# Two key tiles moved behind the first block substitution, one gate tile behind the second, and a later step for the first head's blocks

## The chip, the cores and the metric

The kernel runs on one core of one Trainium2 chip. The metric is the device time of one execution in microseconds (us). TensorE is called PE here, VectorE DVE, ScalarE ACT, GpSimd POOL and SyncE SP, as in the profile.

## The reference, cut to what matters

One decoder layer on 512 tokens of width 2048, all in float32:

```python
u    = rms_norm(x)
proj = u @ w_in                        # 2048 -> 6160 columns
conv = 8 groups of 128 channels: GLU, causal depthwise conv (31 taps), LayerNorm, swish
dn   = 8 heads of 128: short conv (4 taps) + SiLU on q, k, v; gated delta rule in chunks of 64;
       RMSNorm, times silu(z)
h1   = x  + concat(conv, dn) @ w_out
y    = rms_norm(h1 + relu(rms_norm(h1) @ w_up)^2 @ w_down)
```

For each head and chunk the delta rule needs the inverse of a unit lower triangular matrix made of the keys: `t_mat = (I + strict_lower(beta * k k^T * decay))^-1`. With it come `u = t_mat (beta v)` and `w = t_mat (beta k exp(g))`, and then a short recurrence over the chunks. The kernel takes chunks of 128 instead of 64.

## The kernel before, in words

Tokens lie in 4 tiles of 128. Every weight is split into a high and a low part (`whi` by ACT, `wlo` by DVE, lines 157 and 158), and each product is three matmuls (lines 163 to 165). A column tile of the input projection (`in_tile`, 128 columns by 512 tokens) is 48 matmuls of 512 columns. In the trace it is called `pin_` and a letter: a and g for a conv group, q, v, z, k for a head.

The input projection is a list of steps, `ORDER` (line 28). `K3` is head 3's key tile and starts `head_keys(3)`; `I0` inverts the blocks of heads 0 to 3 (`invert_blocks`); `C0` is conv group 0 (tiles a0 and g0); `H0` is delta head 0 (tiles q0 and v0, then z0 for the gate). What follows a tile runs as a generator beside the later tiles. Each `yield n` means: go on after n advances, and `in_tile` makes one advance after every 6 matmuls, 8 to a tile. Starting a second generator of the same kind finishes the one before it (`drain`).

`head_keys` (lines 442 to 481) puts on POOL one product `ug` (line 448, the other half is DVE's), the mask of `dec` (line 459) and a power, `kn` (line 480). The two `ug` of a head feed two matmuls into `pd`; `ug` has a single buffer, so that each next one waits for the matmul of the one before.

`invert_blocks` (lines 483 to 508) writes the four heads' key matrices `na` to DRAM and reads them back as 64 blocks of 32 by 32 (`inv_a`, four DMAs). It runs 31 steps of forward substitution on POOL, two instructions each (lines 503 and 505, 62 in all, on w(j+1) elements with w from 31 to 1), and writes the result to DRAM (`blk_out`). All its DMAs stand in POOL's queue.

`delta_head` (lines 510 to 653) first fetches its four diagonal blocks: a DMA `yc` on POOL, a masked copy `y` on POOL, and four 32-row transposes into `xx` on DVE (line 527). Then follow the short convs of q and v (lines 424 to 435, on ACT and DVE), after `Y_PTQ` = 10 advances the transposes `ptq`, `ptv`, `ptk` on PE, after 13 more (`Y_PX`, first head of a batch) or 1 more (`Y_PX2`, the others) the products `pp`, `pz`, `pp`, `pz` that put the 32-blocks together, then `pw`, `pqk` and the chain over the four chunks.

`conv_group` (lines 379 to 422) is 30 multiply-adds `cacc` on DVE, each of which needs the one before (line 390). They begin when both tiles are there (`chh`), and the PE transposes `cpt` follow them.

Each engine takes its instructions in the order in which they stand in its queue. A scheduler puts them there by program order and `high_priority` offsets and by its own estimate of when each is ready; `pin` keeps the small PE instructions among themselves in program order. A waiting instruction holds up all that stand behind it on its engine.

Of the kernel before, what the change touches and what calls it, by code (L numbers as in the profile page):

```python
# [24 lines left out]
FB = 512  # L25
NROWS = 21
HB = 4
ORDER = "A0 K0 K1 K2 K3 I0 C0 H0 C1 H1 C2 K4 H2 K5 C3 H3 K6 K7 I1 C4 H4 C5 H5 C6 H6 C7 H7"
EPS = 1e-6
DRAW = 5  # L30

# [1 line left out]

NPK, TAPS, Y_PTK, Y_PX2 = 2, 3, 6, 1
S1, S2, S3 = 1, 1, 1
Y_CPT, Y_CPB, Y_PX, Y_POT, Y_PTQ = 14, 8, 13, 4, 10
C_CONF = 0
C_GATE = 1024
C_Q = 2048
# [7 lines left out]
def tile_hybrid_block(ctx: ExitStack, tc: tile.TileContext, x, norm1_w, w_in, b_glu, dw_w, dw_b,  # L47
# [27 lines left out]
    def tt(tag, name, shape=(P, NT, P), dtype=F32, bufs=1):  # L75
        return tmp.tile(list(shape), dtype, tag=tag, name=name, bufs=bufs)
# [4 lines left out]
    def bc(ap):  # L81
        return ap.unsqueeze(2).to_broadcast([P, NT, P])
# [296 lines left out]
    def conv_group(g, pa, pgt):  # L379
        th = tt("c0", f"cth{g}")  # L380
        nc.scalar.activation(fl(th), pgt, AF.Tanh, bias=hgate_c[:, g:g + 1], scale=0.5)
        av = tt("c1", f"cav{g}")
        nc.scalar.activation(fl(av), pa, AF.Identity, bias=bglu_c[:, g:g + 1])
        hh = tt("c2", f"chh{g}", (P, SEQ))
        nc.vector.scalar_tensor_tensor(hh, fl(th), 1.0, fl(av), ALU.add, ALU.mult)
        acc = tt("c3", f"cacc{g}", (P, SEQ))
        nc.scalar.activation(acc, hh, AF.Identity, scale=dw_cols[:, WCONV - 1, g:g + 1],  # L387
                             bias=dwb_c[:, g:g + 1])
        for j in range(1, WCONV):
            nc.vector.scalar_tensor_tensor(acc[:, j:], hh[:, :SEQ - j],  # L390
                                           dw_cols[:, WCONV - 1 - j, g:g + 1], acc[:, j:],
                                           ALU.mult, ALU.add)
# [12 lines left out]
        nc.vector.tensor_scalar(vs, mv[:, :, 1], EPS, None, ALU.add)
        rs = small.tile([P, NT], F32, tag="crs", bufs=2, name=f"crs{g}")
        nc.gpsimd.tensor_tensor(rs, vs, neg_half[:, 0:NT], ALU.pow)
        hn = tt("c4", f"chn{g}")
        for t in range(NT):
            nc.vector.tensor_scalar(hn[:, t], pt[:, t], mv[:, t, 0:1], rs[:, t:t + 1],  # L410
                                    ALU.subtract, ALU.mult)
        yield Y_CPB
        pb = bank(f"cpb{g}")
        for t in range(NT):
            pin(nc.tensor.transpose(pb[:, t], hn[:, t], ident))
        xh = tt("c1", f"cxh{g}")
        nc.scalar.activation(xh, pb, AF.Identity, scale=hlng_c[:, g:g + 1],
                             bias=hlnb_c[:, g:g + 1])
        th2 = tt("c0", f"cth2{g}")
        nc.scalar.activation(th2, xh, AF.Tanh)  # L420
        mixes[g] = row(f"mix{g}")
        nc.vector.scalar_tensor_tensor(mixes[g], fl(th2), 1.0, fl(xh), ALU.add, ALU.mult)

    def short_conv(ps, which, h, tag, acc):
# [9 lines left out]
        nc.vector.scalar_tensor_tensor(acc, th, 1.0, acc, ALU.add, ALU.mult)  # L434
        return acc

    def square_sums(ps, ss, h, name):
        for t in range(NT):
            junk = tt("sj", f"{name}j{h}{t}", (P, P))
            nc.scalar.activation(junk, ps[:, t], AF.Square, accum_out=ss[:, t:t + 1])  # L440

    def head_keys(h, pk):

        pd = bank(f"pd{h}")

        def decay_sums(i):
            ug = tt("ug", f"ug{h}{i}", dtype=F32R)
            (nc.gpsimd, nc.vector)[i].tensor_mul(ug, upper.unsqueeze(1).to_broadcast([P, NT, P]),
                                 bc(glog_split[:, i, :, h]))
            pin(nc.tensor.matmul(fl(pd), lhsT=strict_r, rhs=fl(ug), start=(i == 0), stop=(i == 1)))  # L450

        decay_sums(0)
        k = row(f"k{h}", (P, NT, P))
        short_conv(pk, 1, h, "k", k)
        yield 2
        decay_sums(1)
        dec = row(f"dec{h}", (P, NT, P))
        nc.scalar.activation(dec, pd, AF.Exp)
        nc.gpsimd.tensor_mul(dec, dec, upper.unsqueeze(1).to_broadcast([P, NT, P]))
        yield Y_PTK  # L460
        ptk = bank(f"ptk{h}")
        for t in range(NT):
            pin(nc.tensor.transpose(ptk[:, t], k[:, t], ident))
        kss = small.tile([P, NT], F32, tag="kss", bufs=HB + 1, name=f"kss{h}")
        square_sums(ptk, kss, h, "k")
        nc.vector.tensor_scalar(kss, kss, EPS, None, ALU.add)
        br = small.tile([P, 2, NT], F32, tag="br", bufs=HB + 1, name=f"br{h}")
        nc.vector.reciprocal(br[:, 0], kss)
        nc.vector.tensor_mul(br[:, 0], br[:, 0], beta[:, :, h])
# [12 lines left out]

    def invert_blocks(bt, keys):
# [182 lines left out]
    for op in ORDER.split():  # L666
        kind, r = op[0], int(op[1])
        if kind == "A":

            pabT = ps_mm.tile([P, SEQ], F32, tag="mm", name="pabT")  # L670
            pk = ps_mm.tile([P, SEQ], F32, tag="mm", name="pin_k0")
            ws = [in_weights(C_K, j, "k0", nc.gpsimd, True) for j in range(2)]
            for i in range(2):
                toks = slice(256 * i, 256 * i + 256)
                decay_products(pabT, toks)
                if i:
                    beta, glog_split, eg = decay_columns(pabT)
                for k in range(KT):
                    w = ws[k // 8]
                    mm3(pk[:, toks], (w[0][:, k % 8], w[1][:, k % 8]),  # L680
                        (uT[k][0][:, toks], uT[k][1][:, toks]), start=(k == 0), stop=(k == KT - 1))
        elif kind == "K":
            if r:
                pk = in_tile(C_K + r * P, f"k{r}", nc.gpsimd if r < NPK else nc.vector)
            start(f"key{r}", head_keys(r, pk))
        elif kind == "I":
            drain("key")
            blocks[r] = invert_blocks(r, keys[r * HB:(r + 1) * HB])
        elif kind == "C":
# [318 lines left out]
```

## Time and profile before

| | us |
|---|---|
| median of 3 runs (2214.61 to 2217.39) | 2215.02 |
| the profiled execution | 2217.25 |
| its span | 2215.2 |
| PE busy | 2162.8 |
| DVE busy | 1537.8 |
| ACT busy | 816.0 |
| POOL busy | 226.2 |

The first 40 us load and normalize x. The mixers (ORDER's steps) take until about 720 us, the output projection until about 920 us, the MLP the rest. A change of ORDER touches the stretch from 90 to 720 us alone. PE is the engine to follow: where it has work, the time goes on at its pace, and what another engine costs is seen as PE idle time or as PE at the lower of its two clocks.

### The profile page before, as it was taken

Reading aid. Unit: us, or ns where it says so; the run is one execution under the profiler, and the core shown is the slowest. Engines: PE = TensorE matmul, PEld = TensorE weight load, DVE = VectorE, ACT = ScalarE, POOL = GpSimd, SP = SyncE. Lnnn points to the kernel's source line nnn. Section 1 sums busy time; section 2 is a strip of 40 time slices with the busy share of each in tenths; the row PEclk is TensorE's granted clock in tenths of the full one; section 3 lists DMA queues with packets and bytes.
Section 4 is the critical chain, followed back from the end, with each engine's and each line's share of the span. In section 5 each row is a group of like instructions: output and inputs, shape, how many; then the busy total and the mean of one; then the engine's idle time right before and its main releaser. Section 6 shows DMA issues by size and latency. Waiting matters only on the chain.

```text
span 2215.2 us, 25987 instructions
## 1 busy us (share of the span) xinstructions
PE 2162.8 (98%) x10073; PEld 1791.7 (81%) x10073; DVE 1537.8 (69%) x1956; ACT 816.0 (37%) x1349; POOL 226.2 (10%) x265
## 2 busy tenths in 40 slices
PE   6998999998999999999999999999999999999998
PEld 5877888877888788888888888888888888888886
DVE  6586687586679323477777767767768767768775
ACT  5333433432435323333423424324323423333343
POOL 3382111282100000000000000000000000000000
PEclk9999999999999999999999999999999999999999
DMA  6323233232233633233333233333343333332332
GB/s 164 105 77 75 78 87 90 80 83 73 77 81 86 190 97 94 76 96 117 92 105 114 86 116 103 88 122 95 95 119 95 100 115 95 106 111 89 115 117 84
DMA packets 189768, 220.66 MB, mean 100 GB/s; under 512 B 9901, under 2 KB 108622, under 8 KB 189646
## 3 DMA queue, kind: packets, MB, share of 16 engines
q1 hardware_dynamic: 188238, 215.34, 33.4%
q0 software_dynamic: 1408, 3.67, 0.6%
q8 instruction: 79, 1.29, 0.2%
q14 instruction: 43, 0.35, 0.1%
HBM read 212.17 MB, written 6.82 MB: 99 GB/s over the span
## 4 chain that ended last, share of the span: by engine, by line
PE 88%; POOL 6%; DVE 2%; DMA 2%; issue 1%; ACT 0%; SPq 0%; POOLq 0%; DVEq 0%; ACTq 0%
PE pu L165 10%; PE pu L164 10%; PE pu L163 10%; PE px L164 5%; PE px L165 5%; PE px L163 5%; PE py L164 4%; PE py L163 4%; PE py L165 4%; PE po L163 3%; PE po L165 3%; PE po L164 3%; POOL inv_g L505 2%; POOL inv_t L503 2%; PE pin_k L163 1%
## 5 line engine op out<-in xcount | busy, mean ns | idle before, releaser
L165 PE MATMUL pu<-v_h,wlo_u 128*128 128x512 f32 x1024 | 398.8, 389 | 0.0
L163 PE MATMUL pu<-v_h,whi_u 128*128 128x512 f32 x1024 | 398.4, 389 | 0.0
L164 PE MATMUL pu<-v_l,whi_u 128*128 128x512 f32 x1024 | 398.4, 389 | 0.0
L840 DVE TENSOR_TENSOR wlo_d<-wd,whi_d 128x1024 fp32r<-128x1024 f32 x180 | 218.3, 1219 | 249.8 <-ACT whi_d L839 249.8
L839 ACT CAST whi_d<-wd 128x1024 fp32r<-128x1024 f32 x180 | 189.6, 1054 | 454.7 <-PE pu L164 289.4
L165 PEld LDWEIGHTS pu<-v_h,wlo_u 128*128 128x128 f32 x1024 | 192.2, 188 | 40.1 <-issue 0.2
L163 PEld LDWEIGHTS pu<-v_h,whi_u 128*128 128x128 f32 x1024 | 192.3, 188 | 40.0 <-issue 0.2
L164 PEld LDWEIGHTS pu<-v_l,whi_u 128*128 128x128 f32 x1024 | 192.3, 188 | 39.8
L157 ACT CAST whi_u<-wraw_u 128x1024 fp32r<-128x1024 f32 x128 | 134.8, 1053 | 198.5 <-PE py L165 75.1
L390 DVE SCALAR_TENSOR_TENSOR cacc<-chh,dw_cols,cacc 128x511 f32<-128x511 f32 (+14 forms) x240 | 196.1, 817 | 8.4 <-ACT cacc L387 5.1
L163 PE MATMUL px<-whi_d,sh 128*128 128x512 f32 x480 | 186.7, 389 | 0.0
L164 PE MATMUL px<-wlo_d,sh 128*128 128x512 f32 x480 | 186.7, 389 | 0.0
L165 PE MATMUL px<-whi_d,sl 128*128 128x512 f32 x480 | 186.7, 389 | 0.0
L158 DVE TENSOR_TENSOR wlo_u<-wraw_u,whi_u 128x1024 fp32r<-128x1024 f32 x128 | 155.8, 1217 | 41.2 <-ACT whi_u L157 41.2
L857 DVE TENSOR_TENSOR h<-px,h 128x1024 f32<-128x1024 f32 x120 | 146.5, 1221 | 28.7 <-PE px L165 28.7
L163 PE MATMUL py<-whi_d,sh 128*128 128x512 f32 x360 | 140.0, 389 | 0.0
L164 PE MATMUL py<-wlo_d,sh 128*128 128x512 f32 x360 | 140.0, 389 | 0.0
L165 PE MATMUL py<-whi_d,sl 128*128 128x512 f32 x360 | 140.0, 389 | 0.0
L176 POOL TENSOR_TENSOR rs_rf<-rs_sf,neg_half 128x1 f32<-128x1 f32 x4 | 2.2, 543 | 1309.1 <-DVE rs_sf L174 1309.1
L857 DVE TENSOR_TENSOR h<-py,h 128x1024 f32<-128x1024 f32 x90 | 109.8, 1220 | 22.6 <-PE py L165 22.6
L163 PEld LDWEIGHTS px<-whi_d,sh 128*128 128x128 f32 x480 | 90.1, 188 | 18.7
L165 PEld LDWEIGHTS px<-whi_d,sl 128*128 128x128 f32 x480 | 90.1, 188 | 18.7
(304 smaller groups left out, 4125.5 us busy)
## 6 DMA issues: line engine op xcount, KB each, us to landing
wraw_u<-in_w_mlp_up SPq DMA_DIRECT2D x128, 512.0 KB, 3.7
wd<-in_w_mlp_down SPq DMA_DIRECT2D x120, 512.0 KB, 3.7
wraw_o<-in_w_out SPq DMA_DIRECT2D x32, 512.0 KB, 4.2
wraw_k<-in_w_in SPq DMA_DIRECT2D x16, 512.0 KB, 4.4
wraw_a<-in_w_in SPq DMA_DIRECT2D x16, 512.0 KB, 3.9
wraw_g<-in_w_in SPq DMA_DIRECT2D x16, 512.0 KB, 3.9
wraw_q<-in_w_in SPq DMA_DIRECT2D x16, 512.0 KB, 3.9
wraw_v<-in_w_in SPq DMA_DIRECT2D x16, 512.0 KB, 4.0
```

The source lines that it names most:

```text
L157: nc.scalar.copy(hi, raw)
L158: sub.tensor_sub(lo, raw, hi.bitcast(F32))
L163: nc.tensor.matmul(ps, lhsT=sta[0], rhs=mov[0], start=start, stop=False, skip_group_check=more)
L164: nc.tensor.matmul(ps, lhsT=sta[0], rhs=mov[1], start=False, stop=False, skip_group_check=more)
L165: nc.tensor.matmul(ps, lhsT=sta[1], rhs=mov[0], start=False, stop=stop, skip_group_check=more)
L176: nc.gpsimd.tensor_tensor(rr, s, neg_half[:, 0:1], ALU.pow)
L390: nc.vector.scalar_tensor_tensor(acc[:, j:], hh[:, :SEQ - j], dw_cols[:, WCONV - 1 - j, g:g + 1], acc[:, j:], ALU.mult, ALU.add)
L503: nc.gpsimd.tensor_mul(tv, a[:, j:j + 1, j + 1:].to_broadcast([n, j + 1, w]), g[:, :j + 1, j:j + 1].to_broadcast([n, j + 1, w]))
L505: nc.gpsimd.tensor_add(g[:, :j + 1, j + 1:], g[:, :j + 1, j + 1:], tv)
L839: nc.scalar.copy(hi, src)
L840: nc.vector.tensor_sub(lo, src, hi.bitcast(F32))
L857: nc.vector.tensor_add(h, ps, h)
```

## The change

- In `ORDER`, K4 and K5 stand right behind I0 (before, they stood behind C2 and H2), so that their two tiles and their generators run beside the first substitution. A new step `Z4` (head 4's z tile) stands right behind I1; H4 then skips its own.
- The first head of a batch (heads 0 and 4, `late`) no longer fetches its blocks at its start. The fetch, now the function `block_inverse` with the same instructions, stands 6 advances (`Y_PX` = 6) behind `ptk`, and `pp` 4 advances (`Y_XX` = 4) behind that: 20 advances after the head's start where there were 23. The other heads are as before.
- `ahead()` raises the priority of some POOL instructions (`ug`, `dec`, `kn`, `rt`, `crs`; of `ug` DVE's half too) by 600. `kss`, `br` and `kn` have 6 buffers each instead of 5.

```diff
-ORDER = "A0 K0 K1 K2 K3 I0 C0 H0 C1 H1 C2 K4 H2 K5 C3 H3 K6 K7 I1 C4 H4 C5 H5 C6 H6 C7 H7"
+ORDER = "A0 K0 K1 K2 K3 I0 K4 K5 C0 H0 C1 H1 C2 H2 C3 H3 K6 K7 I1 Z4 C4 H4 C5 H5 C6 H6 C7 H7"
...
-Y_CPT, Y_CPB, Y_PX, Y_POT, Y_PTQ = 14, 8, 13, 4, 10
+Y_CPT, Y_CPB, Y_PX, Y_XX, Y_POT, Y_PTQ = 14, 8, 6, 4, 4, 10
...
+    def ahead():
+
+        return tc.high_priority(offset=600)
...
-        nc.gpsimd.tensor_mul(dec, dec, upper.unsqueeze(1).to_broadcast([P, NT, P]))
+        with ahead():
+            nc.gpsimd.tensor_mul(dec, dec, upper.unsqueeze(1).to_broadcast([P, NT, P]))
...
-    def delta_head(h, key, blocks, pq, pvv):
-        e_c, e_s, e_l = (eg[:, i, :, h] for i in range(3))
-        k, dec, na, kn, br = key
+    def block_inverse(h, blocks):
 
         y = tt("y", f"y{h}")
...
             nc.vector.transpose(xx[rows, :, col:col + 32], yc[rows])
-
+        return y, xx
+
+    def delta_head(h, key, blocks, pq, pvv):
+        e_c, e_s, e_l = (eg[:, i, :, h] for i in range(3))
+        k, dec, na, kn, br = key
+        late = h % HB == 0
+        if not late:
+            y, xx = block_inverse(h, blocks)
...
-        yield Y_PX if h % HB == 0 else Y_PX2
+        if late:
+            yield Y_PX
+            y, xx = block_inverse(h, blocks)
+            yield Y_XX
+        else:
+            yield Y_PX2
...
+        elif kind == "Z":
+            drain("head")
+            gates[r] = z_gate(in_tile(C_Z + r * P, f"z{r}"), r)
         else:
             pq = in_tile(C_Q + r * P, f"q{r}")
             pvv = in_tile(C_V + r * P, f"v{r}")
             start("head", delta_head(r, keys[r], blocks[r // HB], pq, pvv))
-            gates[r] = z_gate(in_tile(C_Z + r * P, f"z{r}"), r)
+            if gates[r] is None:
+                gates[r] = z_gate(in_tile(C_Z + r * P, f"z{r}"), r)
```

POOL's queue from the fetch of the first batch's blocks (`inv_a0`) on, before; the numbers in the names are head, batch and step:

```order
L495 DMA inv_a0_1043<-blk_in0_1041 16x32x32 x4
L503 TENSOR_TENSOR inv_t0_0_1055<-inv_a0_1043,inv_g0_1052 64x31
L505 TENSOR_TENSOR inv_g0_1052<-inv_g0_1052,inv_t0_0_1055 64x31
L503 TENSOR_TENSOR inv_t0_1_1058<-inv_a0_1043,inv_g0_1052 64x60
L505 TENSOR_TENSOR inv_g0_1052<-inv_g0_1052,inv_t0_1_1058 64x2x30
```

The same place now:

```order
L503 DMA inv_a0_1043<-blk_in0_1041 16x32x32
L454 TENSOR_TENSOR ug50_1324<-upper_128,gh_605 128x512
L503 DMA inv_a0_1043<-blk_in0_1041 16x32x32
L466 TENSOR_TENSOR dec4_1247<-dec4_1247,upper_128 128x512
L503 DMA inv_a0_1043<-blk_in0_1041 16x32x32 x2
L488 TENSOR_TENSOR kn4_1321<-kss4_1297,half_136 128x4
L511 TENSOR_TENSOR inv_t0_0_1055<-inv_a0_1043,inv_g0_1052 64x31
L513 TENSOR_TENSOR inv_g0_1052<-inv_g0_1052,inv_t0_0_1055 64x31
L511 TENSOR_TENSOR inv_t0_1_1058<-inv_a0_1043,inv_g0_1052 64x60
L454 TENSOR_TENSOR ug60_3582<-upper_128,gh_605 128x512
L513 TENSOR_TENSOR inv_g0_1052<-inv_g0_1052,inv_t0_1_1058 64x2x30
L511 TENSOR_TENSOR inv_t0_2_1061<-inv_a0_1043,inv_g0_1052 64x87
```

Instructions of heads 4 to 6 now stand among the fetch and the first steps; `dec5` follows the last row shown, and further back in the substitution stand `kn5` and the DMAs that write `na4` and `na5`.

DVE's queue about head 0's v (the last product, which writes the finished `v0`) and its block transposes (`xx0`), before:

```order
L434 SCALAR_TENSOR_TENSOR v0_1449<-vth0_1454,v0_1449 128x512
L390 SCALAR_TENSOR_TENSOR cacc0_1280<-chh0_1278,dw_cols_141,cacc0_1280 128x488
L390 SCALAR_TENSOR_TENSOR cacc0_1280<-chh0_1278,dw_cols_141,cacc0_1280 128x487
L390 SCALAR_TENSOR_TENSOR cacc0_1280<-chh0_1278,dw_cols_141,cacc0_1280 128x486
L390 SCALAR_TENSOR_TENSOR cacc0_1280<-chh0_1278,dw_cols_141,cacc0_1280 128x485
L158 TENSOR_TENSOR wlo_g11_1689<-wraw_g11_1686,whi_g11_1688 128x1024
L390 SCALAR_TENSOR_TENSOR cacc0_1280<-chh0_1278,dw_cols_141,cacc0_1280 128x484
L659 SCALAR_TENSOR_TENSOR z0_1523<-zth0_1521,pin_z0_1457 128x512
L390 SCALAR_TENSOR_TENSOR cacc0_1280<-chh0_1278,dw_cols_141,cacc0_1280 128x483
L527 STREAM_TRANSPOSE xx0_1435<-yc0_1432 32x4x32 x4
L390 SCALAR_TENSOR_TENSOR cacc0_1280<-chh0_1278,dw_cols_141,cacc0_1280 128x482
```

The same queue now, from the multiply-add on 497 columns on:

```order
L390 SCALAR_TENSOR_TENSOR cacc0_1500<-chh0_1498,dw_cols_141,cacc0_1500 128x497
L533 STREAM_TRANSPOSE xx0_1845<-yc0_1842 32x4x32
L390 SCALAR_TENSOR_TENSOR cacc0_1500<-chh0_1498,dw_cols_141,cacc0_1500 128x496
L533 STREAM_TRANSPOSE xx0_1845<-yc0_1842 32x4x32
L390 SCALAR_TENSOR_TENSOR cacc0_1500<-chh0_1498,dw_cols_141,cacc0_1500 128x495
L533 STREAM_TRANSPOSE xx0_1845<-yc0_1842 32x4x32
L390 SCALAR_TENSOR_TENSOR cacc0_1500<-chh0_1498,dw_cols_141,cacc0_1500 128x494
L158 TENSOR_TENSOR wlo_a11_1814<-wraw_a11_1811,whi_a11_1813 128x1024
L390 SCALAR_TENSOR_TENSOR cacc0_1500<-chh0_1498,dw_cols_141,cacc0_1500 128x493
L430 SCALAR_TENSOR_TENSOR v0_1659<-pin_v0_1578,sc_cols_140,v0_1659 128x511
```

Three of the four transposes of `xx0` now stand ahead of all of v0's instructions; the finished `v0` comes 8 rows after the last row shown.

DVE's queue at the same place of the second batch (head 4), now:

```order
L435 SCALAR_TENSOR_TENSOR v4_4291<-vth4_4296,v4_4291 128x512
L390 SCALAR_TENSOR_TENSOR cacc4_4132<-chh4_4130,dw_cols_141,cacc4_4132 128x488
L533 STREAM_TRANSPOSE xx4_4473<-yc4_4470 32x4x32
L390 SCALAR_TENSOR_TENSOR cacc4_4132<-chh4_4130,dw_cols_141,cacc4_4132 128x487
L533 STREAM_TRANSPOSE xx4_4473<-yc4_4470 32x4x32
L390 SCALAR_TENSOR_TENSOR cacc4_4132<-chh4_4130,dw_cols_141,cacc4_4132 128x486
```

Here the transposes still stand behind the finished `v4`; before, six multiply-adds, a weight part and z4 stood between them, as at head 0. On PE, `cpt4` now comes 36 matmuls after `ptk` of head 4 instead of 48 (36 of a5 and 12 of g5), and `cpb4`, the transposes of the normalized group, 16 matmuls after `cpt4` instead of 36.

## Rows read from the trace of the kernel before

**Rows 1.** PE's waits: what waited, for whom: us in total, times, longest.
```profile
PE cpt L398 <- DVE cacc L390: 11.1, 2, 5.7
PE ptv L548 <- DVE v L434: 10.4, 2, 5.3
```
**Rows 2.** PE's timeline, first batch: start us, us, what [idle before, releaser].
```profile
88.79 0.60 PE L463 MATMUL ptk<-ident,k 128*128 128x128 f32 x4
...
90.35 0.40 PE L163 MATMUL pin_a<-u_h,whi_a 128*128 128x512 f32 x1
...
103.22 0.39 PE L163 MATMUL pin_g<-u_h,whi_g 128*128 128x512 f32 x1
...
114.10 0.39 PE L163 MATMUL pin_q<-u_h,whi_q 128*128 128x512 f32 x1
...
149.47 0.60 PE L537 MATMUL ptq<-ident,q 128*128 128x128 f32 x4
155.15 1.12 PE L548 MATMUL ptv<-ident,v 128*128 128x128 f32 x4 [5.09 <-DVE v L434]
...
175.10 1.11 PE L398 MATMUL cpt<-ident,cacc 128*128 128x128 f32 x4 [5.37 <-DVE cacc L390]
...
185.28 1.00 PE L570 MATMUL pp<-xx,na 128*128 128x64 f32 x8
```
**Rows 3.** Five us after a wait: PE PEld DVE ACT POOL, PE clock, DMA share, GB/s.
```profile
155.00:160.00 5.00, 4.85 (x16) 4.18 (x17) 4.89 (x6) 4.36 (x19) 4.61 (x6) 0.50 0.31 92
```
**Rows 4.** PE's timeline, second batch.
```profile
490.06 1.12 PE L548 MATMUL ptv<-ident,v 128*128 128x128 f32 x4 [5.28 <-DVE v L434]
...
510.18 1.12 PE L398 MATMUL cpt<-ident,cacc 128*128 128x128 f32 x4 [5.72 <-DVE cacc L390]
...
520.07 1.00 PE L570 MATMUL pp<-xx,na 128*128 128x64 f32 x8
```
**Rows 5.** DVE's timeline, first batch.
```profile
116.44 0.94 DVE L385 SCALAR_TENSOR_TENSOR chh<-cth,cav 128x512 f32<-128x512 f32 x1
...
139.34 5.44 DVE L390 SCALAR_TENSOR_TENSOR cacc<-chh,dw_cols,cacc 128x497 f32<-128x497 f32 x5
...
154.02 1.08 DVE L434 SCALAR_TENSOR_TENSOR v<-vth,v 128x512 f32<-128x512 f32 x1
...
173.05 1.24 DVE L527 STREAM_TRANSPOSE xx<-yc 32x128 f32<-32x128 f32 x4 [10.55 <-DMA yc<-blk_out]
```
**Rows 6.** POOL's timeline: head 2's key instructions, then the first batch's substitution.
```profile
92.01 1.40 POOL L480 TENSOR_TENSOR kn<-kss,half 128x4 f32<-128x4 f32 x1 [7.89 <-DVE kss L466]
...
94.41 1.28 POOL L459 TENSOR_TENSOR dec<-dec,upper 128x512 f32<-128x512 f32 x1
...
111.86 0.23 POOL L503 TENSOR_TENSOR inv_t<-inv_a,inv_g 64x31 f32<-64x31 f32 x1 [4.76 <-DMA inv_a<-blk_in]
...
126.79 0.92 POOL L503 TENSOR_TENSOR inv_t<-inv_a,inv_g 64x231 f32<-64x231 f32 x1
...
134.28 0.67 POOL L505 TENSOR_TENSOR inv_g<-inv_g,inv_t 64x252 f32<-64x252 f32 x1
...
145.35 1.54 POOL L505 TENSOR_TENSOR inv_g<-inv_g,inv_t 64x247 f32<-64x247 f32 x1
...
165.22 0.27 POOL L505 TENSOR_TENSOR inv_g<-inv_g,inv_t 64x31 f32<-64x31 f32 x1
```
**Rows 7.** POOL's timeline, first and last instruction of the second batch's substitution.
```profile
446.90 0.23 POOL L503 TENSOR_TENSOR inv_t<-inv_a,inv_g 64x31 f32<-64x31 f32 x1 [4.89 <-DMA inv_a<-blk_in]
...
500.13 0.27 POOL L505 TENSOR_TENSOR inv_g<-inv_g,inv_t 64x31 f32<-64x31 f32 x1
```
**Rows 8.** DVE's timeline at head 5, where POOL does little.
```profile
561.78 1.21 DVE L158 TENSOR_TENSOR wlo_g<-wraw_g,whi_g 128x1024 fp32r<-128x1024 f32 x1
562.91 0.71 DVE L390 SCALAR_TENSOR_TENSOR cacc<-chh,dw_cols,cacc 128x486 f32<-128x486 f32 x1
563.55 0.73 DVE L429 SCALAR_TENSOR_TENSOR v<-pin_v,sc_cols,v 128x509 f32<-128x509 f32 x1
```

More of the change, by code (lines that the diff above doesn't have):

```diff
@@ L406, in conv_group @@
         rs = small.tile([P, NT], F32, tag="crs", bufs=2, name=f"crs{g}")
-        nc.gpsimd.tensor_tensor(rs, vs, neg_half[:, 0:NT], ALU.pow)
+        with ahead():
+            nc.gpsimd.tensor_tensor(rs, vs, neg_half[:, 0:NT], ALU.pow)
         hn = tt("c4", f"chn{g}")
@@ L447, in decay_sums @@
             ug = tt("ug", f"ug{h}{i}", dtype=F32R)
-            (nc.gpsimd, nc.vector)[i].tensor_mul(ug, upper.unsqueeze(1).to_broadcast([P, NT, P]),
-                                 bc(glog_split[:, i, :, h]))
+            with ahead():
+                (nc.gpsimd, nc.vector)[i].tensor_mul(ug, upper.unsqueeze(1).to_broadcast([P, NT, P]),
+                                                     bc(glog_split[:, i, :, h]))
             pin(nc.tensor.matmul(fl(pd), lhsT=strict_r, rhs=fl(ug), start=(i == 0), stop=(i == 1)))
@@ L458, in head_keys @@
         nc.scalar.activation(dec, pd, AF.Exp)
-        nc.gpsimd.tensor_mul(dec, dec, upper.unsqueeze(1).to_broadcast([P, NT, P]))
+        with ahead():
+            nc.gpsimd.tensor_mul(dec, dec, upper.unsqueeze(1).to_broadcast([P, NT, P]))
         yield Y_PTK
@@ L463, in head_keys @@
             pin(nc.tensor.transpose(ptk[:, t], k[:, t], ident))
-        kss = small.tile([P, NT], F32, tag="kss", bufs=HB + 1, name=f"kss{h}")
+        kss = small.tile([P, NT], F32, tag="kss", bufs=HB + 2, name=f"kss{h}")
         square_sums(ptk, kss, h, "k")
         nc.vector.tensor_scalar(kss, kss, EPS, None, ALU.add)
-        br = small.tile([P, 2, NT], F32, tag="br", bufs=HB + 1, name=f"br{h}")
+        br = small.tile([P, 2, NT], F32, tag="br", bufs=HB + 2, name=f"br{h}")
         nc.vector.reciprocal(br[:, 0], kss)
@@ L478, in head_keys @@
                                            ALU.mult, ALU.mult)
-        kn = small.tile([P, NT], F32, tag="kn", bufs=HB + 1, name=f"kn{h}")
-        nc.gpsimd.tensor_tensor(kn, kss, half, ALU.pow)
+        kn = small.tile([P, NT], F32, tag="kn", bufs=HB + 2, name=f"kn{h}")
+        with ahead():
+            nc.gpsimd.tensor_tensor(kn, kss, half, ALU.pow)
         keys[h] = (k, dec, na, kn, br)
@@ L540, in delta_head @@
         rt = small.tile([P, NT], F32, tag="rt", bufs=2, name=f"rt{h}")
-        nc.gpsimd.tensor_tensor(rt, ss, neg_half[:, 0:NT], ALU.pow)
+        with ahead():
+            nc.gpsimd.tensor_tensor(rt, ss, neg_half[:, 0:NT], ALU.pow)
         cq = small.tile([P, 2, NT], F32, tag="cq", bufs=2, name=f"cq{h}")
```

## The prediction

> **What bounds the kernel now.** I read the views in this order: the page's busy times, PE's waits, then the timelines of PE, DVE and POOL about each wait. PE is busy for nearly the whole span, so a change of ORDER can gain only what PE loses to waits and to its lower clock. PE's waits beyond the start are four: twice `ptv` waits for head 0's or 4's v, twice `cpt` for the last multiply-add of a conv group [rows 1]. All lie about the two block substitutions. In the first batch they end at 155.15 and 175.10 us [rows 2]. After such a wait the granted clock is 0.50 for about 5 us, the lower of the two levels (1.2 of 2.4 GHz) [rows 3]; PE had stood idle before it.
>
> The loss of the first batch: from `ptq` at 149.47 to `pp` at 185.28 are 35.8 us [rows 2]. The work there is 78 matmuls at 10.88 / 48 = 0.227 us (a tile goes from 103.22 to 114.10 [rows 2]), 17.7 us, and four groups of four transposes, some 0.45 each (an estimate: ptk, pkk and pd take 1.56 us together, 88.79 to 90.35 [rows 2]), 1.8 us. So 16.3 us are lost: 10.5 in the two waits, 5.8 in the clock and the restarts, which I call 2.7 a wait (2.5 to 2.9). The second batch is the first one 335 us later: `ptv`, `cpt`, `pp`, the substitution's start and end all stand 334.8 to 335.1 us behind their partners [rows 2, 4, 6, 7]. Both batches together lose 32.6 us; that is all there is to gain, 1.5%.
>
> Why PE waits. POOL's 62 substitution instructions run from 111.86 to 165.5 [rows 6], and beside them DVE is slow: `cacc` takes 1.09 us apiece (5.44 for five [rows 5]) against 0.64 start to start where POOL rests [rows 8]. So v is late, the first wait. The second: the block transposes stood 10.55 us in DVE's queue waiting for the DMA `yc` [rows 5], and the last `cacc` stood behind them.
>
> **The change in the first batch.** K4 and K5 add nothing to PE; they come earlier. Each brings a tile (10.88), ptk, pkk and pd (1.56) and the second pd (0.3): all that follows moves by 2 x 12.75 = 25.5 us, the conv's start on DVE too, from 116.44 [rows 5] to 141.9. PE then reaches `ptv` at 149.92 + 25.5 = 175.4.
>
> POOL pays first. K4's and K5's instructions stand in its queue ahead of the substitution, `kn4` above all. It needs `ptk4`, which PE reaches after K4 (103.2, where a0 ended), pd, 48 matmuls and pd, at 114.7. Head 2's `kn` began 3.2 us after its `ptk` [rows 2, 6], so `kn4` begins at 117.9 and ends at 119.1. The substitution begins there instead of at 111.86 [rows 6]. After three of its instructions (0.9) comes `ug60`, which needs pd5's second matmul (119.3, in time; 1.1 us), then two more (0.8) and `dec5` (1.28 [rows 6]): 123.3. What is left: alone, an instruction takes 0.17 + 0.002 us per element (0.23 for 31, 0.67 for 252 [rows 6]) and some 0.07 to the next. All 62 have 10,912 elements, 37 us; less the five done (1.8), plus `kn5` (1.2) and the issues of `na4` and `na5` (1.3), 37.7 us are left.
>
> Beside a full DVE it stretches: the 17 instructions from 126.79 to 145.35 [rows 6] would take 12.6 us alone and took 18.6, a factor of 1.5. Beside K4 and K5 no row shows it. DVE is then about half busy, so I take 1.2, with the ends 1.0 and 1.5. From 123.3 to 141.9 that does 15.5 us of the 37.7. Then DVE is full with the conv, until it has issued the `cacc` on 497 columns, at 139.34 + 1.1 + 25.5 = 165.9: 24.0 / 1.5 = 16.0 more. 6.2 us are left.
>
> Now the order decides. Right behind that `cacc` stands the first transpose of `xx0`, and it waits for `yc`. Before, the transposes stood behind v and most of the conv; now all of v0 is behind them. DVE stands still from 165.9. POOL, undisturbed, ends at 172.1; from there to DVE's go took 7.6 us (165.5 to 173.05 [rows 5, 6]): 179.7. Behind it stand three transposes (0.9), eight `cacc` and three of v's products at 0.65 (7.2), two weight parts at 1.13 (2.3 [rows 8]) and v's last product (0.7), with 0.4 for POOL's `y`: v0 is there at 191.2. PE has waited since 175.4: 15.8 us, plus one restart, 2.7. After it the conv is ahead of PE, so the second wait is gone. The batch loses 18.5 us against 16.3: **+2.2**. With the factor 1.0 POOL ends at 169.0 (-0.9), with 1.5 at 175.2 (+5.3). Each us of POOL is a us of PE here. Later in the batch `pp` comes three advances earlier, which costs nothing: `xx0` and `y` are 12 us old by then.
>
> **The change in the second batch.** z4 moves from behind v4 to a place beside the substitution's start: the conv and `ptv` both come 10.9 us later, POOL doesn't. The rows between `chh` and v4 on DVE are the same and still beside POOL, so the first wait stays: v4 at 154.02 + 1.08 + 335 + 10.9 = 501.0, `ptv` reached at 495.8, 5.2 us and a restart: 7.9. The second shrinks. For the first 15.4 us POOL has only four short DVE instructions beside it, does 13.4 us of its 37 and ends at 497.7 by the factor 1.5; the same reckoning ends the first batch some 2 us early, so I take 499.2. `yc` is there at 506.8, the transposes and six `cacc` with a weight part take 6.4, and `cpt4` can go at 513.2. Undisturbed PE would be there at 495.8 + 0.9 + 8.2 = 504.9: 8.3 us lost, nearly the first wait alone. New: `cpb4` comes 16 matmuls behind `cpt4` where 36 were enough: between 0 and 20 x 0.227 = 4.5 us, taken as 1.2, since only a statistics chain stands between. And head 4's chain runs one tile later, so `pot4` comes 16 matmuls behind the last chunk where 24 were enough: 0 to 1.8, taken as 1.5, because conv 5 now crowds DVE there. 11.0 against 16.3: **-5.3**. Ends: 7.0 (both new waits nil and DVE a little quicker at the substitution's end), -9.3; and 17.3 (a second restart and both new waits whole), +1.0.
>
> **At no cost:** head pairs C2 H2 and C3 H3 without K4 and K5 between them follow the pattern of C6 H6 C7, where PE had no wait; weights come on SP in the new order with the same lead. If that cover fails, a late weight costs PE its lateness, 1 us or so. The sixth buffers and `ahead` change POOL's order only where told.
>
> **The sum.** +2.2 - 5.3 = -3.1, between -10.2 and +6.3. From the profiled execution, 2217.25, that is 2214.2; the median was 2.2 us under the profiled one, so 2212.0.
>
> **Rivals.** A, *faster*: the substitution is hardly disturbed beside K4 and K5, and the new waits of the second batch don't come: -0.9 - 9.3 = -10.2, 2204.8. For it: DVE's work there is half from PSUM. Against it: the first wait of the second batch has no reason to go.
>
> B, *the change does what it looks to be for*: the substitutions are covered and no wait is left, -32.6, 2182.4. Against it: even undisturbed POOL ends at 123.3 + 37.7 = 161.0, `yc` is there at 168.6 and v0 at 180.1, after PE. It would need `kn4` and the rest to cost POOL nothing.
>
> C, *slower*: DVE blocks POOL more beside the key tiles than the rows of before show. Each us goes straight to PE's wait at `ptv`; from a substitution that ends at 179.6 (7.5 us behind my 172.1) the time is over 0.2% up. If POOL and DVE took turns, the 8.5 us of DVE work that reads two tiles from SBUF in 123.3 to 141.9 would leave POOL 10.1, the next 24.0 us would give 13.2 (the 17 instructions above would need 12.6 and DVE's 11.7 beside them 24.3 instead of 18.6), and the end is 180.2: +10.3 - 5.3 = +5.0, 2220.0. The row speaks against it: 18.6 us is less than turns allow. The Trainium skill ("SBUF — State Buffer", section "SBUF: two separate sides") calls the port pair that DVE and GpSimd share an exclusive lock, by which a DVE instruction with two SBUF inputs and a GpSimd instruction that reads SBUF run in turn; by that rule the time is C's, and the trace agrees only in part.
>
> **How the numbers follow.** A measurement of this kernel tells about 0.2%, 4.4 us, from no change. The forecast (no change by that measure) has 0.50, A 0.33, B 0.04, C 0.13: faster 0.37, same 0.50, slower 0.13. The range is the sum's own, taken from the median: 2215.0 - 10.2 = 2204.8 and 2215.0 + 6.3 = 2221.3, so 2205 to 2221; outside it lie B and the far side of C.
>
> **What would show it.** Right: one PE wait of some 16 us at `ptv` near 175 us, DVE idle for some 14 us before a transpose of `xx0`, `kn4` waiting ahead of the substitution; in the second batch a wait of some 5 us at `ptv` and one of under 3 at `cpt`. Wrong: two waits in the first batch as before, or `yc` back before 168, or new waits of PE between 200 and 430 us or behind 515 us.

## The result

The changed kernel takes 2244.65 us (median of 4 runs, 2243.12 to 2246.22) against 2214.82 us before: a ratio of 1.0133, interval 1.0115 to 1.0150. It is 30 us slower, where the forecast was 2212.0 with a range of 2205 to 2221.

The profiled span grew from 2215.2 to 2241.4 us, by 26.2; the profiled executions, 2217.25 us before and 2243.12 after, lie at the upper and the lower end of their kernels, hence 26 and not 30. The page's first lines after the change, with PE's busy time:

```profile
span 2241.4 us, 25993 instructions
PE 2182.0 (97%) x10073; PEld 1792.5 (80%) x10073; DVE 1537.7 (69%) x1956; ACT 814.5 (36%) x1349; POOL 216.1 (10%) x265
```

PE is busy for 19 us more than before, and the change gave it no work. So most of the loss isn't idle time. Two landmarks on PE, behind which both kernels have the same work left, divide it: head 3's `ptq`, behind the first batch, and `pr`, just before the MLP. First the kernel before, then after:

```profile
390.64 0.60 PE L537 MATMUL ptq<-ident,q 128*128 128x128 f32 x4
...
898.71 1.10 PE L769 MATMUL pr<-r_diag,ones 128*128 128x512 f32 x2 [0.52 <-DVE r_diag L767]
```
```profile
394.50 0.60 PE L550 MATMUL ptq<-ident,q 128*128 128x128 f32 x4
...
902.67 1.10 PE L792 MATMUL pr<-r_diag,ones 128*128 128x512 f32 x2 [0.50 <-DVE r_diag L790]
```

The mixers lost 3.9 us in the first batch and nothing more until the MLP (4.0). The other 22.2 us are lost in the MLP, whose code the change doesn't touch. There PE has no gap and its granted clock is 1.00 in both; it only does fewer matmuls in the same time. A stretch of 100 us in the MLP (us, then PE, PEld, DVE, ACT, POOL busy with instructions, PE clock, DMA share, GB/s), before and after:

```profile
1300.00:1400.00 100.00, 100.00 (x443) 82.84 (x442) 75.54 (x72) 34.86 (x42) 0.00 (x0) 1.00 0.32 96
```
```profile
1300.00:1400.00 100.00, 100.00 (x436) 81.63 (x435) 72.50 (x70) 34.39 (x42) 0.00 (x0) 1.00 0.33 100
```

By tile, the loss sits in the down projection, `px` and `py`, whose stationary tiles are `sh` and `sl` (the high and low halves of the hidden rows; the stationary operand is the one that an LDWEIGHTS row loads, the other operand of a matmul is called the moving one). Duration min/median/max in ns of their weight loads and matmuls, before and after:

```profile
L163 PEld LDWEIGHTS px<-whi_d,sh x480: 187/188/188, 949.3 to 2161.8; 128*128 128x128 f32 x160
L163 PE MATMUL px<-whi_d,sh x480: 389/389/389, 949.6 to 2162.0; 128*128 128x512 f32 x160
```
```profile
L163 PEld LDWEIGHTS px<-whi_d,sh x480: 186/188/193, 953.3 to 2186.7; 128*128 128x128 f32 x160
L163 PE MATMUL px<-whi_d,sh x480: 391/396/401, 953.5 to 2186.9; 128*128 128x512 f32 x160
```

From start to start (mean over 1000 to 1900 us) a matmul on `px` or `py` takes 226.7 ns before and 234.1 after, one on `pu` 226.7 and 227.6. There are 2520 and 3072 of them: 18.6 + 2.8 = 21.4 of the 22.2 us. (The operands of `pu` moved in no byte, and no run explains its 0.9 ns.)

In the mixers the change did nearly what was forecast. PE's waits after (in total, times, longest), and its timeline in the first batch with the new waits in brackets:

```profile
PE ptv L562 <- DVE v L435: 19.9, 2, 16.5
PE cpt L398 <- DVE cacc L390: 4.2, 1, 4.2
PE pot L670 <- POOL o L666: 3.0, 2, 2.0
```
```profile
174.34 0.60 PE L550 MATMUL ptq<-ident,q 128*128 128x128 f32 x4
191.42 1.12 PE L562 MATMUL ptv<-ident,v 128*128 128x128 f32 x4 [16.48 <-DVE v L435]
...
208.97 1.00 PE L589 MATMUL pp<-xx,na 128*128 128x64 f32 x8
```

The two waits of the first batch [rows 2] have become one of 16.48 us. DVE and POOL beside it:

```profile
165.80 1.00 DVE L390 SCALAR_TENSOR_TENSOR cacc<-chh,dw_cols,cacc 128x497 f32<-128x497 f32 x1
179.78 0.30 DVE L533 STREAM_TRANSPOSE xx<-yc 32x128 f32<-32x128 f32 x1 [12.98 <-DMA yc<-blk_out]
...
190.69 0.67 DVE L435 SCALAR_TENSOR_TENSOR v<-vth,v 128x512 f32<-128x512 f32 x1
```
```profile
117.67 1.03 POOL L488 TENSOR_TENSOR kn<-kss,half 128x4 f32<-128x4 f32 x1 [7.39 <-DVE kss L473]
118.69 0.23 POOL L511 TENSOR_TENSOR inv_t<-inv_a,inv_g 64x31 f32<-64x31 f32 x1
...
171.74 0.27 POOL L513 TENSOR_TENSOR inv_g<-inv_g,inv_t 64x31 f32<-64x31 f32 x1
```

DVE stands still for 13 us before a transpose that waits for `yc`, and v, which PE waits for, is queued behind it. In the second batch both waits of before [rows 4] are still there, shorter, and the clock is again 0.50 behind the second (the last row covers 518 to 523 us):

```profile
503.42 0.67 PE L562 MATMUL ptv<-ident,v 128*128 128x128 f32 x4 [3.43 <-DVE v L435]
...
518.53 1.12 PE L398 MATMUL cpt<-ident,cacc 128*128 128x128 f32 x4 [4.20 <-DVE cacc L390]
...
559.60 0.66 PE L670 MATMUL pot<-ident,o 128*128 128x128 f32 x4 [2.03 <-POOL o L666]
```
```profile
511.35 0.30 DVE L533 STREAM_TRANSPOSE xx<-yc 32x128 f32<-32x128 f32 x1 [7.34 <-DMA yc<-blk_out]
```
```profile
518.00:523.00 5.00, 4.46 (x13) 3.70 (x14) 3.80 (x11) 0.00 (x0) 1.17 (x2) 0.50 0.38 109
```

### The profile page after: what moved, and what is told of

Same layout as the page of the kernel before. It is cut to its first block, busy times and chain, and to the rows that moved or that the text cites. A ratio compares the mean times of both kernels' runs of the same rounds, so it can differ in the third digit from the quotient of the medians.

```text
span 2241.4 us, 25993 instructions
## 1 busy us (share of the span) xinstructions
PE 2182.0 (97%) x10073; PEld 1792.5 (80%) x10073; DVE 1537.7 (69%) x1956; ACT 814.5 (36%) x1349; POOL 216.1 (10%) x265
## 4 chain that ended last, share of the span: by engine, by line
PE 87%; POOL 6%; DVE 3%; DMA 2%; issue 2%; ACT 1%; SPq 0%; POOLq 0%; DVEq 0%; ACTq 0%
PE pu L164 10%; PE pu L163 10%; PE pu L165 10%; PE px L164 5%; PE px L165 5%; PE px L163 5%; PE py L164 4%; PE py L165 4%; PE py L163 4%; PE po L165 3%; PE po L163 3%; PE po L164 2%; POOL inv_g L513 2%; POOL inv_t L511 2%; DVE cacc L390 1%
## 5 line engine op out<-in xcount | busy, mean ns | idle before, releaser
L390 DVE SCALAR_TENSOR_TENSOR cacc<-chh,dw_cols,cacc 128x511 f32<-128x511 f32 (+14 forms) x240 | 187.8, 782 | 6.7 <-ACT cacc L387 3.3
L164 PEld LDWEIGHTS px<-wlo_d,sh 128*128 128x128 f32 x480 | 90.6, 189 | 21.6
```

Source lines behind the costliest of these rows:

```text
L164: nc.tensor.matmul(ps, lhsT=sta[0], rhs=mov[1], start=False, stop=False, skip_group_check=more)
```

## Experiments on the MLP: the place of the tiles

What of the change can reach the MLP is the place of its tiles in SBUF, the memory on the chip in which every tile takes the same bytes of its partitions. The sixth buffers of `kss`, `br` and `kn` lie in the pool `small`, each in a slot of 32 bytes of every partition; all pools behind it, the MLP's among them, move by 3 x 32 = 96 bytes. As the programs lay them down, `sh` and `sl` begin at byte 179648 before and 179744 after, and the tiles of weights and activations, which lie ahead of `small`, don't move. I first took multiples of 64 for what counts (theory P: 179648 is one, 179744 is 32 beyond), against a loss through anything else in the program (theory Q).

**e1**: the kernel before with an unused tile made larger, which moves everything behind `small` by 32 bytes.

```diff
-    small.tile([P, 8], F32, tag="small_filler", bufs=1, name="small_filler")
+    small.tile([P, 16], F32, tag="small_filler", bufs=1, name="small_filler")
```

> The kernel before with one unused tile of the pool `small` 32 bytes larger, and nothing else: the order of all instructions is the old one, and every tile behind that pool lies 32 bytes further on in SBUF, 32 beyond a multiple of 64, as the change leaves it (there they lie 96 bytes further). Theory P (place: the matmuls of the MLP's down projection are slower because their stationary tiles sh and sl begin 32 bytes beyond a multiple of 64): the start to start of these matmuls goes from 226.7 to 234 ns, the MLP takes 22 us more, the whole 2215 + 22 = 2237 us. Theory Q (the MLP is slower through something else of the changed program: its order, its length, its transfers, the clock): 226.7 ns, 2215 us.

Measured: 2236.27 us against 2217.04, ratio 1.0088 (1.0074 to 1.0102), 233 ns on `px` and `py`; `pr` came at 898.78, as before. An unused tile, with the order of instructions the old one, costs 19 us, all of it in the MLP. Theory Q can't account for that.

**e2**: the same line in the changed kernel.

> The changed kernel with the same unused tile 32 bytes larger, so that the tiles behind the pool lie 128 bytes further on than before, on multiples of 64 again. Theory P: the MLP is as before, 226.7 ns a matmul; what is left is the 4.0 us by which the changed kernel reached the MLP late, so 2219 us (2217 to 2221). Theory Q: 2244.6 us, as the changed kernel.

Measured: 2238.51 us against 2217.04, 1.0097 (1.0082 to 1.0113). Theory P was wrong here: at 128 bytes, a multiple of 64, `px` and `py` still take 232.9 ns.

```profile
1300.00:1400.00 100.00, 100.00 (x436) 81.81 (x435) 72.72 (x71) 33.85 (x42) 0.00 (x0) 1.00 0.33 100
```

**e3**: the kernel before, with only `sh` and `sl` moved.

```diff
+            if fb == 0 and i == 0:
+                mlp.tile([P, 8], F32, tag="pad0", name="pad0")
             hi = mlp.tile([P, 2, 256], F32R, tag=f"sh{i}", name=f"sh{fb}_{i}")
...
             p4 = split(a22, 6)
+            if fb == 0:
+                mlp.tile([P, 8], F32, tag="pad1", name="pad1")
```

> The kernel before with 32 unused bytes ahead of the fourteen tiles sh and sl and 32 behind them: these alone lie 32 bytes beyond a multiple of 64, everything else lies where it did. Theory P: the matmuls on px and py take 234 ns, those on pu 226.7, and the time is 2520 x 7.3 ns = 18.4 us up, 2233.4 us (with pu's 1 ns as well, if that comes from sh and sl too, 2236.5). Rival (it is another moved tile: wd, h, r_rows, or the tiles of the mixers): no change, 2215 us.

Measured: 2235.90 us, 1.0086 (1.0072 to 1.0099): as much as e1. (The expectation was inexact in one point: the `wd` tiles behind them, which PE doesn't read, moved by 64 bytes.) So it is `sh` and `sl`, and e2 shows that the step of 64 isn't it. What then?

**e5**: the changed kernel with every tile of the MLP at its old byte.

```diff
-    small.tile([P, 8], F32, tag="small_filler", bufs=1, name="small_filler")
...
-    alog = small.tile([P, NH], F32, tag="alog", bufs=1, name="alog")
+    alog = mixc.tile([P, NH], F32, tag="alog", bufs=1, name="alog")
...
-    dtb = small.tile([P, NH], F32, tag="dtb", bufs=1, name="dtb")
+    dtb = mixc.tile([P, NH], F32, tag="dtb", bufs=1, name="dtb")
```

> The changed kernel with the pool `small` as large as before: its unused tile is left out (32 bytes) and the two 32-byte tiles alog and dtb lie in another pool, so that every tile of the MLP lies at exactly the byte where it lay before; the order of instructions is that of the change. e1 and e3 moved tiles alone and lost some 19 us in the MLP; e2 put them on multiples of 64 again, 128 bytes further, and kept that loss, so a multiple of 64 is not the point. Theory P2 (the place of sh and sl itself decides, and the old one is free of the loss): 226.7 ns a matmul in the MLP, and 4 us over the kernel before from the mixers: 2219 to 2221 us. Theory Q (the program after the change is slower in the MLP wherever its tiles lie): 2238 us, as e2.

Measured: 2220.33 us against 2216.48, ratio 1.0020 (1.0011 to 1.0028), 226.7 ns: theory P2. The change's own effect on the mixers is +3.9 us; the rest of its 30 us is the place.

**e7, e8, e11**: e3 with `pad0` of 64, 512 and 256 bytes (and no `pad1`), one execution each.

> The kernel before with sh, sl (and the wd tiles behind them) 64 bytes further on, nothing else. What is asked is the start to start of the matmuls on px and py, 226.7 ns before. If only steps under 64 bytes cost something: 226.7. If 64 bytes cost like 32, 96 and 128 did: 232 to 235 ns, 19 us more in all.

> The same with 512 bytes, the size of one stationary slice in a partition. If the loss comes from how the place of the stationary slice stands to that of the moving tile, counted modulo 512 or less: 226.7 ns, the time of before. If it is the absolute place, or counted modulo more: 232 to 235 ns and 19 us more.

> The kernel before with sh and sl (and the wd tiles behind them) 256 bytes further on. 512 bytes cost nothing (226.7 ns a matmul), 32, 64, 96 and 128 cost 6 to 7.5 ns. If the place counts modulo 256: 226.7 ns. If modulo 512: 232 to 235 ns.

Measured: 2237.11, 2215.79 and 2215.81 us. The same 100 us of e7, then of e8:

```profile
1300.00:1400.00 100.00, 100.00 (x436) 81.58 (x435) 72.02 (x69) 33.82 (x42) 0.00 (x0) 1.00 0.32 96
```
```profile
1300.00:1400.00 100.00, 100.00 (x443) 82.80 (x442) 75.08 (x72) 34.41 (x43) 0.00 (x0) 1.00 0.33 99
```

| `sh`, `sl` moved by, bytes | ns on `px`, `py` | run |
|---|---|---|
| 0 | 226.7 | before, e5 |
| 32 | 233.1 | e1, e3 |
| 64 | 233.5 | e7 |
| 96 | 234.1 | after |
| 128 | 232.9 | e2, e4 |
| 256, 512 | 226.7 | e11, e8 |

Of the shifts tried, the multiples of 256 cost nothing and all others about 3%; none between 128 and 256 was tried here. Before, `sh`, `sl`, the weights and the activations all begin 192 bytes beyond a multiple of 256.

**e12, e13**: the kernel before with 64 unused bytes ahead of all tiles (e12), and between the activations and the weights (e13), one execution each.

```diff
-    const.tile([P, 8], F32, name="const_filler")
+    const.tile([P, 24], F32, name="const_filler")
```
```diff
+    gap = ctx.enter_context(tc.tile_pool(name="gap", bufs=1))
+    gap.tile([P, 16], F32, name="gap_filler")
     w_pool = ctx.enter_context(tc.tile_pool(name="wp", bufs=4))
```

> The kernel before with 64 unused bytes ahead of all its tiles, so that every tile, the weights and the activations too, lies 64 bytes further on. If what counts is how the stationary slice lies to the moving tile that is read beside it: nothing changes between them, 226.7 ns in the MLP and the time of before. If the absolute place of sh and sl counts: 232 to 235 ns on px and py, as with 64 bytes for them alone.

> The kernel before with 64 unused bytes between the pool of the activations (u, v, m: the halves of x, of the normalized rows and of the mixers' output) and that of the weights: weights and everything behind them, sh and sl among it, lie 64 bytes further on, the activations where they lay. Theory R (what counts is how the stationary tile lies to the moving tile of the same matmuls): px and py, whose two tiles have moved together, stay at 226.7 ns; the up projection pu, whose stationary is a weight and whose moving tile an activation, goes to 233 ns, and so do the input and output projections, in all some 2300 + 770 + 3070 matmuls x 6 to 7 ns = 35 to 45 us, 2252 to 2260 us. Theory T (the partner is another tile, not the moving one): everything at 226.7 ns, 2216 us.

Measured: e12 2212.58 us and 226.7 ns on `px`, `py` and `pu`; e13 2248.06 us against 2213.99. In e13 the loss has changed sides: `pu` takes 233.3 ns from start to start, `px` and `py` 227.5. The groups of e13 (busy us, mean ns of one):

```profile
L167 PE MATMUL pu<-v_h,wlo_u 128*128 128x512 f32 x1024 | 404.0, 395 | 0.0
L165 PE MATMUL pu<-v_h,whi_u 128*128 128x512 f32 x1024 | 403.6, 394 | 0.0
...
L165 PE MATMUL px<-whi_d,sh 128*128 128x512 f32 x480 | 187.0, 390 | 0.0
```

`px` and `py` take their stationary tile from `sh` and `sl` and the moving one from the weights, which moved together; `pu` takes the stationary one from the weights and the moving one from the activations, which moved apart. So the absolute place doesn't count (e12), but how the stationary tile lies to the moving one (theory R). The loss was smaller than the 35 to 45 us I expected, because the input and output projections lost less: `pr` came 7.8 us late (906.51). In the input projection, whose stationary tiles are weights as in `pu`, a matmul of an undisturbed tile (`pin_z`) did go from 226.7 to 233.3 ns, and part of that was taken off the waits (at `ptv` 7.8 us in all instead of 10.4). The output projection `po` is another case. Its stationary tiles are the activations and the moving ones the weights. So in e13 its stationary tile lies 64 bytes below the old distance, where in the table above it lies 32 to 128 bytes beyond it. Its 768 matmuls took 195.6 us from the first start to the last instead of 194.1, 1.9 ns more apiece and not 6 to 7. So 64 bytes one way don't cost what 64 bytes the other way cost; whether the direction alone makes the difference, no run shows.

## Experiments on the mixers: DVE's order

Theory O: what PE waits for after the change is the transposes' place in DVE's queue, 13.0 and 7.3 us of waiting for `yc` with v or the last `cacc` behind them. The rival: the substitution on POOL sets both.

**e4** and **e6**: the changed kernel with the transposes of the first head kept behind the last multiply-add, in e4 with the tiles as in e2, in e6 at their old bytes as in e5. Ahead of each transpose one column of the finished `cacc` is copied into the block of `xx` that the transpose then overwrites; so the transposes can't be put ahead of it.

```diff
+        accs[g] = acc
...
             rows = slice(32 * block, 32 * block + 32)
+            if h % HB == 0:
+                nc.vector.tensor_copy(xx[rows, 0, col:col + 1], accs[h][rows, SEQ - 1:SEQ])
             nc.vector.transpose(xx[rows, :, col:col + 32], yc[rows])
```

> The changed kernel on multiples of 64 as in e2, and in both batches the four block transposes into xx of the first head are kept behind the last multiply-add of the conv group by four copies of one column from cacc into xx ahead of them (0.1 us each), so that no multiply-add and no product of v waits behind them on DVE. Theory O (the 13.0 and 7.3 us of DVE's wait for yc are what PE waits for at ptv in the first batch and at cpt in the second): v of head 0 comes at about 179 instead of 191.3, PE's wait at ptv falls from 16.5 to about 5 us, cpt of the second batch no longer waits (4.2 us before); with the clock 12 + 7 us less than e2, about 2200 us (2197 to 2207). Rival S (the substitution's length on POOL sets both, through yc and pp): the waits move to pp, and the time is that of e2 within 3 us.

Measured: 2221.02 us, 17.5 less than e2 (expected 19), though the MLP ran at 232.9 ns. `pr` came at 882.10: 20.6 us ahead of the changed kernel and 16.6 ahead of the kernel before.

> e4 (the transposes of xx kept behind the last multiply-add) with the MLP's tiles at exactly the bytes where they lay before, as in e5. e4 reached the MLP 16.6 us ahead of the kernel before and lost some 20 us in it. Theory P2: 226.7 ns a matmul, 16.6 us less than before: 2199 to 2201 us. Theory Q: as e4, 2221 us.

Measured: 2203.35 us against 2216.48, ratio 0.9941 (0.9928 to 0.9955), some 2 us over the range expected. This version beats both kernels. Its waits, and the first batch on PE and DVE:

```profile
PE ptv L564 <- DVE v L435: 6.4, 2, 3.3
PE pot L672 <- POOL o L668: 3.0, 2, 2.1
```
```profile
179.13 0.66 PE L564 MATMUL ptv<-ident,v 128*128 128x128 f32 x4 [3.13 <-DVE v L435]
...
194.20 1.00 PE L591 MATMUL pp<-xx,na 128*128 128x64 f32 x8
```
```profile
178.39 0.68 DVE L435 SCALAR_TENSOR_TENSOR v<-vth,v 128x512 f32<-128x512 f32 x1
...
185.78 0.32 DVE L534 COPY xx<-cacc 32x1 f32<-32x1 f32 x2
...
187.42 0.63 DVE L535 STREAM_TRANSPOSE xx<-yc 32x128 f32<-32x128 f32 x2 [1.12 <-DMA yc<-blk_out]
```

v is there at 179.1 (expected 179) instead of 191.4, the waits at `cpt` are gone, and `pp`, the reader of `xx`, doesn't wait: the last transpose is done at 190.6. POOL ended 4.5 us later than after the change (176.5), beside a DVE that no longer stood still, and that cost nothing.

**e9, e10**: e6 with the old ORDER, and e6 without `Z4` alone. They ask whether the moved tiles are needed at all.

```diff
-ORDER = "A0 K0 K1 K2 K3 I0 K4 K5 C0 H0 C1 H1 C2 H2 C3 H3 K6 K7 I1 Z4 C4 H4 C5 H5 C6 H6 C7 H7"
+ORDER = "A0 K0 K1 K2 K3 I0 C0 H0 C1 H1 C2 K4 H2 K5 C3 H3 K6 K7 I1 C4 H4 C5 H5 C6 H6 C7 H7"
```
```diff
-ORDER = "A0 K0 K1 K2 K3 I0 K4 K5 C0 H0 C1 H1 C2 H2 C3 H3 K6 K7 I1 Z4 C4 H4 C5 H5 C6 H6 C7 H7"
+ORDER = "A0 K0 K1 K2 K3 I0 K4 K5 C0 H0 C1 H1 C2 H2 C3 H3 K6 K7 I1 C4 H4 C5 H5 C6 H6 C7 H7"
```

> e6 with the old ORDER: K4 and K5 behind C2 and H2 and no Z4 step, but the later fetch of the first head's blocks, the transposes of xx kept behind the last multiply-add, and the MLP's tiles at their old bytes. Asked is whether e6's gain is that of the moved tiles or that of DVE's order. Theory M (the moved tiles are needed: without them the substitution is not covered, v waits 5 us as before, and pp, which needs xx and comes about 12 us earlier, takes over the wait that cpt had): within 4 us of the kernel before, 2213 to 2219 us. Theory D (it is all DVE's order): cpt's two waits of 5.4 and 5.7 us go with their clock loss of 2.7 each, PE waits some 2 us at pp, 12 us less, 2202 to 2206 us, as e6.

> e6 without the step Z4: K4 and K5 moved, the transposes late, head 4's z tile behind its v tile as before. The first batch should be that of e6 (10.8 us ahead of the kernel before at head 3's ptq, 379.8 us). In e6 the second batch gave 5.6 us more. Theory M: without z4 beside its start the second substitution ends as late against PE as before, and PE waits at ptv (5 us) and pp: the second batch gives 0 to 2 us, 2205 to 2208 us. Theory D: it gives 5 to 6 us all the same, 2202 to 2204 us.

Measured: e9 2224.06 us, ratio 1.0034 (1.0021 to 1.0047), slower than before; e10 2211.82, 0.9981 (0.9971 to 0.9990). PE's waits in e9:

```profile
PE pp L591 <- DVE xx L605: 10.5, 2, 6.0
PE ptv L564 <- DVE v L435: 9.6, 2, 5.0
PE pp L591 <- DVE xx L535: 4.3, 2, 2.2
```

DVE in e9, first batch:

```profile
173.13 0.63 DVE L535 STREAM_TRANSPOSE xx<-yc 32x128 f32<-32x128 f32 x2 [9.51 <-DMA yc<-blk_out]
...
182.50 1.22 DVE L157 TENSOR_TENSOR wlo_v<-wraw_v,whi_v 128x1024 fp32r<-128x1024 f32 x1
183.63 0.59 DVE L602 COPY y<-pz 32x128 f32<-32x128 f32 x2
184.25 0.30 DVE L605 STREAM_TRANSPOSE xx<-y 32x128 f32<-32x128 f32 x1
```

and PE's waits in e10:

```profile
PE ptv L564 <- DVE v L435: 8.5, 2, 5.4
PE pp L591 <- DVE xx L605: 6.0, 1, 6.0
```

Theory M, and further than it went (both times lie above its ranges): without the moved tiles nothing covers the substitution, the wait moves from `cpt` to `pp`, and to the second `pp`, which needs a later step of `xx` (184.25) that stands on DVE behind the work held up by the 9.51 us. In e10 that is so in the second batch alone. So, with DVE's order mended, K4 and K5 are worth 12 us (e9 to e10) and `Z4` another 8 (e10 to e6, each against the executions of before beside it).

## Why the prediction was wrong

- **The step that failed** is the line under "At no cost": "The sixth buffers and `ahead` change POOL's order only where told." I took three small buffers for a matter of POOL's order and didn't ask where they put the tiles behind them. They moved `sh` and `sl` by 96 bytes, and the sum lacked a term of 22 us (e1, e3, e5, e13). No rival had it either. That a change of ORDER touches the stretch from 90 to 720 us alone was true of ORDER, but the change was more than that; and the loss showed neither as PE idle time nor as a lower clock, the two places where I looked for one. The code names two unused tiles "filler"; that something hung on addresses could have been asked.
- **The first batch** came out by its steps: `kn4` at 117.67 to 118.7 (forecast 117.9 to 119.1), the substitution's end at 172.0 (172.1), DVE's go at 179.78 (179.7), v at 191.4 (191.2), a wait of 16.48 us (15.8). The two factors by which DVE stretches POOL came as taken: by the prediction's own times for POOL alone, some 1.2 up to 142.4 us and some 1.5 from there to 167.2. The batch lost 3.9 us against a forecast of 2.2, within its bounds; 0.9 of the rest is a new wait at head 0's `pot`, which I had looked for in the second batch alone.
- **Rival C's price** (DVE and POOL in turns, the end at 180.2) didn't come: 172.0. But turns themselves are in the rows of before, POOL's first, then DVE's:

```profile
134.28 0.67 POOL L505 TENSOR_TENSOR inv_g<-inv_g,inv_t 64x252 f32<-64x252 f32 x1
...
136.07 1.75 POOL L505 TENSOR_TENSOR inv_g<-inv_g,inv_t 64x255 f32<-64x255 f32 x1
```
```profile
134.29 1.20 DVE L390 SCALAR_TENSOR_TENSOR cacc<-chh,dw_cols,cacc 128x499 f32<-128x499 f32 x1
...
136.07 1.21 DVE L158 TENSOR_TENSOR wlo_a<-wraw_a,whi_a 128x1024 fp32r<-128x1024 f32 x1
```

  At 134.28 POOL takes the 0.67 us that it takes alone and DVE's `cacc` 1.20 instead of some 0.7; at 136.07 DVE takes its 1.21 [rows 8] and POOL 1.75 instead of some 0.7. Of two that start together, one runs as alone and the other is held. The Trainium skill ("SBUF — State Buffer", section "SBUF: two separate sides") calls the shared port pair an exclusive lock, and these rows agree with it. What failed is C's price. It counted every instruction whole, while 24.3 us of such work fitted into 18.6, and it counted 8.5 us of two-input DVE work beside K4 and K5, where the trace after the change has some 5. (Its 13.2 us for the next 24.0 should also be 24.0 x 12.6 / 24.3 = 12.4.)
- **The second batch** was forecast at -5.3 and gave between +0.1 (after) and -1.4 (e5, `pr` at 901.19). The mechanism was right, the term of the `cpt` wait was too small: I let one restart stand for both waits, but the second, of 4.20 us where my sum left 8.3 - 7.9 = 0.4, had its own (clock 0.50 from 518 to 523), which I had kept for the upper end. The wait at `ptv` was 3.43 us for 5.2, that at `pot` 2.03 for 1.5, and none came at `cpb` after the change (1.2). With 2.7 for the restart, the prediction's figure, these make -5.3 + 3.8 + 2.7 - 1.8 + 0.5 - 1.2 = -1.3, an estimate that agrees with e5.
- **The sum of the mixers**, -3.1, between -10.2 and +6.3, was +3.9 by e5 (interval 2.4 to 6.2): inside those bounds, with the sign wrong, at the edge of the 0.2% that a measurement tells from no change. The time left the range by the MLP alone.
- **Rival B** (all waits gone) has no support in the change as it stands; in e6, with one more constraint on DVE, 13 of its 32.6 us came.

## What to carry to other kernels

When an edit adds or resizes any tile, ask which tiles behind it move and by how many bytes, the two operands of the largest matmul loops first; a few unused bytes can restore the place, and a loss in code that the edit doesn't touch, with a busy PE at full clock, points there. When a kernel moves work to cover a long chain on another engine, look at what stands in the in-order queues right behind the instruction that waits for the chain's end: here the cover was worth 20 us only once that instruction stood behind the work that PE needed first.

## What the hardware showed that was not expected

- A matmul of 512 columns takes 226.7 ns from start to start when its stationary and its moving tile lie a multiple of 256 bytes apart, and 233 to 234 when the stationary one lies 32, 64, 96 or 128 bytes beyond that (e1, e3, e7, e2, the changed kernel, and e13 on `pu`). With the stationary tile 64 bytes short of it, in `po` of e13, the price was 1.9 ns. The weight loads keep their 188 ns; the matmuls go from 389 to 396. Why is not shown: that the two reads of PE disturb each other is the reading that fits e12 and e13. Products whose two tiles hadn't moved against each other also took up to 1 ns more in the slow kernels (`pu` 227.6 after the change, `px` and `py` 227.5 in e13), which is open. The Trainium skill ("SBUF — State Buffer", section "A bandwidth-pool intuition that's wrong (but worth ruling out)") gives PE a second, independent read port for the weights; by the runs here the pace of a matmul does depend on how the two operands lie.
- The length of a PE wait didn't decide what clock followed it. A wait of 3.13 us at head 0's `ptv` left 1.00 over the next 5 us in e6 and 0.66 in e10; waits of 4.95 and 4.65 us in e9 gave 0.66, those of over 4 us in the kernel before and after the change 0.50. The same wait in e6, then in e10:

```profile
179.13:184.13 5.00, 5.00 (x26) 4.30 (x27) 4.89 (x7) 4.93 (x20) 0.31 (x2) 1.00 0.52 138
```
```profile
178.87:183.87 5.00, 5.00 (x19) 4.32 (x20) 4.89 (x7) 4.32 (x19) 0.30 (x2) 0.66 0.51 138
```
